# The output phase of a hybrid trunk: norms as 2 KB pieces, and the input added through PSUM by ScalarE

## The chip, the cores and the metric

One core of a Trainium2 chip runs the whole program. The time is that of the device, in microseconds (us), the median of several runs: lower is better. The engines are PE (TensorE: matmuls; PEld its weight loads), DVE (VectorE), ACT (ScalarE), POOL (GpSimd) and SP (SyncE, which here issues nearly all DMAs, in order). Each engine works through its own queue in order, and waits at an instruction whose inputs or buffers aren't ready; what stands behind it waits as well.

## What is computed

One layer over 2048 positions of width 1024, all in float32:

```
h    = rmsnorm(x);  proj = h @ w_in                 # split into u_b u_c u_h z xbc dt
y_a  = u_b * conv3(u_c * u_h)                       # short convolution mixer, 1024 wide
y    = ssd_scan(conv4(xbc), dt) + d_skip * xs       # chunked state-space scan, 16 heads
y_b  = rmsnorm over each of 2 groups of 512 (y * silu(z))
x    = x + concat(y_a, y_b) @ w_out                 # the output phase
x    = x + square(relu(rmsnorm(x) @ w_up)) @ w_down
out  = rmsnorm(x)
```

The change is in the line of the output phase, and in how the norms of y_b come to it.

## The kernel before

Everything lies transposed: 128 channels on the partitions, positions along the free axis. The 2048 positions are 4 blocks b of 512, the 1024 output channels 8 tiles d of 128. Matmuls work on float32r operands split into a high and a low part, so each product of a weight block and an activation block is three matmuls of 512 columns (L118 to L120 in `mm3`, L315 to L317 in `chain`).

**Pairs.** The half of the output projection that takes y_a comes first. `Output.pair(p)` for p = 0 to 7 computes two output tiles for two position blocks at once, c11, c12, c21 and c22, by the seven products of a Strassen-Winograd scheme instead of eight. Each product (b11, t1, t2, b21, t3, b22, t4, in this order) is 4 blocks of 3 matmuls. They accumulate in three PSUM banks: b11 goes to bank x and is copied by ACT into bank w (the copy `pw<-px`, L322), t1 goes to bank y, t2 adds to x, b21 adds to w, t3 adds to x, b22 adds to y, t4 adds to x. So t3 may not start until x has been read after t2, t4 not until it has been read after t3, and the next pair's t1 takes the bank that t4 filled. Banks x and y come in turn from the three banks k0, k1 and k2, bank w is k3.

After a product, `evict` (in `pair`) reads the bank. Before the pair, `begin` has loaded four tiles of the input x (`xt<-x`, `facc<-x`, L1602; 256 KB each); the six evictions add the bank to these tiles on DVE (L1627), the sums go out to x1_d in DRAM (`x_d<-xt`, `x_d<-facc`, L1630). The tiles of pair 0 come from a pool of the phase before (`begin(0, ...)` in `second_half`). The buffers are three of tag xt and two of tag facc.

**Units.** The half that takes y_b follows: `Output.unit(n)` for n = 32 to 63, one output tile d of one block b each, 8 k-blocks of 3 matmuls into one bank `pm` (in turn k0, k1, k2). The unit before has loaded x1_d for it (`residual`, `xt<-x_d`, L1658); DVE adds (L1679) and the result goes back to x1_d (L1680). For blocks 0 and 1 ACT squares the result (L1692) for the next norm.

**The scan beside it.** During the pairs and the first 16 units the state-space scan of blocks 2 and 3 is still running, a generator whose steps the function `hook` takes after every product and twice per unit: loads (`xd`, `bc`, `dec`, `eb`, `y`), transposes on PE (`ptx`, `ptb`), the copy `xtok<-ptx` (L1418) and the cast `xtok<-stmp` (L1434) on ACT, eight decays per chunk on ACT (`dec`, L1433), and so on. So the scan's instructions stand in the same queues as the pairs' and units'. `dec` is a broadcast of 512 KB from rd_d, `eb` two broadcasts of 128 KB each. The order on each engine is the program's, rearranged in places by the framework's scheduler before the kernel is built.

**The norms.** When a block and group of the scan is done, four small matmuls (`pn`, L1488) sum the squares over 512 channels; each of the block's four chunks of 128 positions gets its own 32 partitions, all with the same sums. ACT and DVE make the reciprocal root r of 128 x 128, and the whole tile is stored to rn_d (`rn_d<-ssq`, L1494; 64 KB). `norm` reads it back (`rn<-rn_d`, L1511): from rows 0, 32, 64 and 96 of rn_d, 512 bytes each, broadcast to 128 partitions (256 KB). `scale` multiplies y_b by it (L1571), `fill` splits it (ACT L1580, DVE L1581), each at a place of `hook` that `schedule` fixes by hand: for the four blocks the loads are at places 46, 54, 70 and 93 (7 places per pair, then 2 per unit with unit n at 2n).

Of the kernel before, what the change touches and what calls it, by code (L numbers as in the profile page):

```python
# [11 lines left out]
F32 = mybir.dt.float32  # L12
# [28 lines left out]
def trunk(ctx: ExitStack, tc: tile.TileContext, x, w_in, w_dt, w_out, w_up, w_down, cvec, hrow, out):  # L41
# [19 lines left out]
    ym_d = seven("ym")  # L61
    wide = lambda n, k: [dram.tile([P, k, TH], F32, name=f"{n}_d{h}") for h in range(2)]
    xs_d, sz_d, yn_d = wide("xs", 12), wide("sz", 8), wide("yn", 8)
    rn_d = [[dram.tile([P, L], F32, name=f"rn_d{b}_{g}") for g in range(G)] for b in range(NB)]
    dt_d = [dram.tile([P, 4, NC * 16], F32, name=f"dt_d{b}") for b in range(NB)]
    rd_d = [dram.tile([2, NC * 16, P], F32, name=f"rd_d{b}") for b in range(NB)]
    pd_d = dram.tile([P, TB], F32, name="pd_d")
# [406 lines left out]
    class Proj(Seven):  # L474
# [429 lines left out]
        def second_half(self, ws, side, stack):  # L904

            self.dt_open()
            dts = itertools.chain(*(self.dt_part(NBB + bb) for bb in range(NBB)))
            count = itertools.count()
            for m, what in enumerate(self.LATER):
                last = m + 1 == len(self.LATER)  # L910
                if m + 2 == len(self.LATER):
                    for _ in side:
                        pass
                    stack.close()
                    rb = stack.enter_context(tc.tile_pool(name="rb", bufs=1, reuse_waits="tile"))
                    self.fresh = lambda n: rb.tile([P, 2, TB], F32, tag="rb", name=n, bufs=4)
                    self.stored = ym_d
                    self.new = [{} for _ in range(4)]
                if last:
                    sums_d["o0"] = "none"  # L920
                    ahead = self.pairs(w_out[0], (0, 1), "o0", True)
                else:
                    ahead = self.weights(1, self.LATER[m + 1])

                def after(name):
                    if m or name == "t4":
                        next(dts, None)
                    for _ in range(1 + (next(count) % 3 == 2)):
                        next(side, None)
                    if m + 2 == len(self.LATER) and name == "t3":  # L930
                        self.got = self.fetch(0, 0)
                    if last:
                        if name == "t1":
                            next(ahead)
                        if name != "b11":
                            self.refresh(name, 0)
                        if name == "b22":
                            proj_out.begin(0, lambda tag: rb.tile([P, TB], F32, tag="xt", name="xt", bufs=4))

                ws = self.pair(1, what, ws, ahead, after)  # L940
            self.places = self.new
            return ws
# [396 lines left out]
    class Scan:  # L1339
# [104 lines left out]
        def back(self, n):  # L1444

            b, g, c, h, ts, r0 = self.place(n)
            t = self.got.pop(n)
            cT = t["bc"][:, 1]
            byhead = lambda a: a.rearrange("p (h d) -> p h d", h=HG)
            state = self.state[g]  # L1450
            st = psum("tp", "st", 2)
            mm3(st, *t["btok"], *t["parts"], 0, 1)
            yo = psum("k4", "yo")
            for j in range(4):
                nc.tensor.matmul(yo[:, j * L : (j + 1) * L], state[:, j * P : (j + 1) * P], cT, start=True, stop=True)
            yd = t["yd"]
            for i in range(HG):
                nc.tensor.matmul(
                    yd[(i % 2) * 64 : (i % 2) * 64 + 64, (i // 2) * L : (i // 2 + 1) * L],
                    byhead(t["xdt"])[:, i, :],  # L1460
                    t["dec"][:, i % 2 * 4 + i // 2, :],
                    start=False,
                    stop=True,
                    skip_group_check=True,
                )
            y = t["y"]
            t1 = self.tmp()
            nc.vector.tensor_tensor(out=byhead(state), in0=byhead(state), in1=t["cdec"], op=ALU.mult)
            nc.vector.tensor_tensor(out=state, in0=state, in1=st, op=ALU.add)
            nc.vector.tensor_tensor(out=t1, in0=yo, in1=t["eb"].rearrange("p j l -> p (j l)"), op=ALU.mult)  # L1470
            nc.vector.tensor_tensor(out=t1, in0=t1, in1=yd, op=ALU.add)
            yield
            t3 = t1.rearrange("p (j l) -> p j l", j=4)
            nc.vector.tensor_tensor(out=y, in0=t3, in1=y, op=ALU.mult)
            yield
            nc.sync.dma_start(yn_d[h][:, 4 * g : 4 * g + 4, ts], y)
            q4 = self.tmp().rearrange("p (j l) -> p j l", j=4)
            self.act = nc.scalar.activation(q4, y, AF.Square)
            nc.vector.tensor_tensor(out=q4[:, 0:2], in0=q4[:, 0:2], in1=q4[:, 2:4], op=ALU.add)
            if c == 0:  # L1480
                self.ssq = self.tile([TB], "ssq", 1)
            ssq = self.ssq
            nc.vector.tensor_tensor(out=ssq[:, c * L : (c + 1) * L], in0=q4[:, 0], in1=q4[:, 1], op=ALU.add)
            yield
            if c == NC - 1:
                pn = psum("tp", "pn", 2)
                for i in range(NC):
                    nc.tensor.matmul(  # L1488
                        pn[i * 32 : i * 32 + 32, 0:L], ones[:, 0:32], ssq[:, i * L : (i + 1) * L], start=True, stop=True
                    )  # L1490
                r = ssq[:, 0:L]
                nc.scalar.activation(r, pn[:, 0:L], AF.Sqrt, bias=eps, scale=1.0 / 512)
                nc.vector.reciprocal(out=r, in_=r)
                nc.sync.dma_start(rn_d[b][g], r)  # L1494
            yield
            yield

# [2 lines left out]
        def norm(self, b, g):  # L1500

            if (b, g) not in self.rn:
# [4 lines left out]
                else:  # L1507
                    t = uh.tile([P, TB], F32, tag="uh3", name="rn", bufs=4)
                self.rn[b, g] = t
                row = rn_d[b][g].rearrange("(q p) l -> p q l", p=32)[0]  # L1510
                nc.sync.dma_start(t.rearrange("p (q l) -> p q l", q=NC), row.partition_broadcast(P))  # L1511
            return self.rn[b, g]

        def run(self, begin, end):
# [34 lines left out]
    class Output:  # L1549
# [34 lines left out]

        def open(self, stack, ws):
            self.xp = stack.enter_context(tc.tile_pool(name="xp", bufs=1, reuse_waits="tile"))
            self.xt = {}
            self.start_ws = ws
            proj.fresh = self.raw

# [1 line left out]
            return self.xp.tile([P, 2, TB], F32, tag="ry", name=name, bufs=4)  # L1592

        def small(self, tag):
            return self.xp.tile([P, TB], F32, tag=tag, name=tag, bufs={"xt": 3, "facc": 2}[tag])

        def begin(self, p, tile=None):

            t = self.begun = {}
            for name, (b, i, tag) in self.TILES.items():  # L1600
                t[name] = (tile or self.small)(tag)
                nc.sync.dma_start(t[name], x[p // 4 * 2 + b, :, p % 4 * 2 + i])  # L1602

        def pair(self, p, hook):

            tiles = self.begun
            last = p == 7
            if p == 3:
                proj.new = [{} for _ in range(4)]
# [5 lines left out]
                ahead = proj.pairs(w_out[0], (d, d + 1), f"o{p + 1}", True)  # L1615

            def evict(name, gi, pm):
                for c, acc, end in {
                    "t1": (("c22", "y", 0),),
                    "t2": (("c12", "x", 0),),  # L1620
                    "b21": (("c11", "w", 1),),
                    "t3": (("c22", "x", 1),),
                    "b22": (("c12", "y", 1),),
                    "t4": (("c21", "x", 1),),
                }.get(name, ()):
                    t = tiles[c]
                    nc.vector.tensor_tensor(out=t, in0=pm[acc], in1=t, op=ALU.add)  # L1627
                    if end:
                        b, i, _ = self.TILES[c]
                        nc.sync.dma_start(x1_d[p // 4 * 2 + b][:, p % 4 * 2 + i], t)  # L1630

            def after(name):
                n = ("b11", "t1", "t2", "b21", "t3", "b22", "t4").index(name)
                if name == "b22":
                    if last:
                        self.residual(32)
                    else:
                        self.begin(p + 1)
                if p == 2 and name == "t4":
                    proj.got = proj.fetch(0)  # L1640
                if p == 3:
# [12 lines left out]
        def residual(self, n):  # L1654
            if n < len(self.UNITS):
                i, b, d = self.UNITS[n]
                t = self.xt[n] = self.small("xt")
                nc.sync.dma_start(t, x1_d[b][:, d])  # L1658

        def weights(self, m):  # L1660
            if m < 2 * KD and m not in self.ws:
                self.ws[m] = split_src(w_out[1, m % KD])

        def unit(self, n, hook):
# [3 lines left out]
            m = b // 2 * KD + d  # L1668
            if b % 2 == 0:
                self.weights(m + 2)  # L1670
            pm = psum("mm", "pm")
            whi, wlo = self.ws[m]
            for j in range(KD):
                if j == KD // 2:
                    hook(2 * n)
                k = j // 2 + j % 2 * 4
                mm3(pm, whi[:, k, :], wlo[:, k, :], *self.y[i, b][k], j, KD)
            t = self.xt.pop(n)
            nc.vector.tensor_tensor(out=t, in0=pm, in1=t, op=ALU.add)  # L1679
            nc.sync.dma_start(x1_d[b][:, d], t)  # L1680
# [38 lines left out]
    with ExitStack() as c1:  # L1719
# [17 lines left out]
        with ExitStack() as c2:  # L1737
# [13 lines left out]

            for p in range(8):
                proj_out.pair(p, hook)
            for n in range(32, 48):
                proj_out.unit(n, hook)
            for _ in side:
# [95 lines left out]
```

## Time and profile before

| | |
|---|---|
| median of 3 runs | 2622.15 us (2621.07 to 2628.47) |
| the profiled execution | 2623.34 us, of it the span 2621.6 us |
| mean granted PE clock | 0.993 |
| PE busy over the span | 2577.2 us (98%) |
| DVE, ACT busy over the span | 1946.4 us (74%), 1408.8 us (54%) |
| output phase, pairs (first to last eviction) | 970.9 to 1164.1 us |
| output phase, units (first to last addition) | 1181.2 to 1376.5 us |

Busy time is the time in which an engine executes; a wait shows as idle time, and the view names what ended it. PE's clock is granted by the chip, 1.00 being full speed.

### The profile page before, as it was taken

To read this page: it belongs to the slowest core of one execution; us is meant where nothing else is said; L and a number is where in the kernel's file an instruction comes from. 1 tells how busy PE (TensorE), PEld (TensorE's weight loads), DVE (VectorE), ACT (ScalarE), POOL (GpSimd) and SP (SyncE) were. 2 spreads that over 40 slices of the span, in tenths; PEclk is the share of its full clock that TensorE was granted. 3 is DMA by queue.
4 is the path that set the end of the run, shared out by engine and by line. 5 is a ranking of instruction groups with operands and counts; after the bars stand their busy time and mean duration, and the time that the engine had idled before them with its cause. 6 is when DMAs were issued, how large, how long until landed. Compare 5 with 4: busy or idle time off the path is not lost.

```text
span 2621.6 us, 33756 instructions
## 1 busy us (share of the span) xinstructions
PE 2577.2 (98%) x12027; PEld 2115.4 (81%) x12027; DVE 1946.4 (74%) x2651; ACT 1408.8 (54%) x2135; POOL 77.1 (3%) x99
## 2 busy tenths in 40 slices
PE   9999999999999999979999999999999999999998
PEld 7888878788888777767788888888888888888787
DVE  7877877878786778977777775744448887888885
ACT  6554345876676656554335555755556444444443
POOL 2110010000000000000000000000000000000001
PEclk9999999999999999989999999999999999999999
DMA  4555665756656478887666786765557554665762
GB/s 171 176 189 189 218 231 196 230 188 202 191 180 197 152 276 264 285 232 233 206 209 240 258 317 245 261 229 181 212 186 258 183 182 154 213 208 180 236 209 77
DMA packets 263016, 553.35 MB, mean 211 GB/s; under 512 B 27072, under 2 KB 99520, under 8 KB 262848
## 3 DMA queue, kind: packets, MB, share of 16 engines
q1 hardware_dynamic: 262272, 550.29, 62.4%
q8 instruction: 94, 1.54, 0.2%
q10 hardware_dynamic: 576, 0.92, 0.1%
q14 instruction: 74, 0.61, 0.1%
HBM read 364.20 MB, written 186.91 MB: 210 GB/s over the span
## 4 chain that ended last, share of the span: by engine, by line
PE 77%; DMA 7%; DVE 7%; ACT 5%; issue 3%; SPq 0%; POOL 0%; POOLq 0%; DVEq 0%; ACTq 0%
PE px L315 13%; PE px L317 13%; PE px L316 13%; PE py L315 6%; PE py L316 6%; PE py L317 6%; PE pw L315 3%; PE pw L317 3%; PE pw L316 3%; DMA dec<-rd_d 3%; PE pm L118 2%; PE pm L120 2%; PE pm L119 2%; ACT dec L1433 1%; DVE wlo L104 1%
## 5 line engine op out<-in xcount | busy, mean ns | idle before, releaser
L315 PE MATMUL px<-uh,whi 128*128 128x512 f32 x1800 | 705.8, 392 | 7.9 <-DVE xt L1627 2.4
L317 PE MATMUL px<-uh,wlo 128*128 128x512 f32 x1800 | 701.3, 390 | 0.0
L316 PE MATMUL px<-ul,whi 128*128 128x512 f32 x1800 | 701.0, 389 | 0.0
L315 PEld LDWEIGHTS px<-uh,whi 128*128 128x128 f32 x1800 | 337.9, 188 | 86.8 <-issue 4.1
L317 PEld LDWEIGHTS px<-uh,wlo 128*128 128x128 f32 x1800 | 337.9, 188 | 72.5 <-issue 2.2
L316 PEld LDWEIGHTS px<-ul,whi 128*128 128x128 f32 x1800 | 338.1, 188 | 68.9 <-issue 0.2
L104 DVE TENSOR_TENSOR wlo<-wraw,whi 128x512 fp32r<-128x512 f32 (+1 forms) x213 | 217.0, 1019 | 206.5 <-ACT whi L103 205.5
L315 PE MATMUL py<-uh,whi 128*128 128x512 f32 x900 | 353.0, 392 | 3.1 <-DVE facc L1627 2.6
L317 PE MATMUL py<-uh,wlo 128*128 128x512 f32 x900 | 351.4, 390 | 0.0
L316 PE MATMUL py<-ul,whi 128*128 128x512 f32 x900 | 351.3, 390 | 0.0
L103 ACT CAST whi<-s 128x1024 fp32r<-128x1024 f32 x226 | 236.5, 1047 | 204.8 <-PE py L316 86.8
L103 ACT CAST whi<-wraw 128x1024 fp32r<-128x1024 f32 (+1 forms) x214 | 190.5, 890 | 278.0 <-PE px L316 224.1
L104 DVE TENSOR_TENSOR wlo<-s,whi 128x1024 fp32r<-128x1024 f32 x226 | 275.1, 1217 | 80.3 <-ACT whi L103 79.7
L315 PEld LDWEIGHTS py<-uh,whi 128*128 128x128 f32 x900 | 169.4, 188 | 42.2 <-issue 5.7
L317 PEld LDWEIGHTS py<-uh,wlo 128*128 128x128 f32 x900 | 169.4, 188 | 35.4 <-issue 0.2
L316 PEld LDWEIGHTS py<-ul,whi 128*128 128x128 f32 x900 | 169.3, 188 | 35.4 <-issue 0.8
L315 PE MATMUL pw<-uh,whi 128*128 128x512 f32 x450 | 176.3, 392 | 0.0
L317 PE MATMUL pw<-uh,wlo 128*128 128x512 f32 x450 | 175.3, 390 | 0.0
L316 PE MATMUL pw<-ul,whi 128*128 128x512 f32 x450 | 175.1, 389 | 0.0
L391 DVE TENSOR_TENSOR ul<-rh,uh 128x1024 fp32r<-128x1024 f32 (+1 forms) x128 | 138.7, 1087 | 33.1 <-ACT uh L390 32.9
L390 ACT CAST uh<-rh 128x1024 fp32r<-128x1024 f32 (+1 forms) x128 | 120.3, 943 | 74.6 <-PE py L317 60.5
L118 PE MATMUL pm<-uh,whi 128*128 128x512 f32 (+1 forms) x392 | 150.2, 384 | 0.7 <-ACT z L601 0.7
(264 smaller groups left out, 3599.1 us busy)
## 6 DMA issues: line engine op xcount, KB each, us to landing
hid_d<-e SPq DMA_DIRECT2D x96, 512.0 KB, 3.5
rh<-hid_d SPq DMA_DIRECT2D x96, 512.0 KB, 4.3
wraw<-w_in SPq DMA_DIRECT2D x68, 512.0 KB, 4.2
wraw<-w_down SPq DMA_DIRECT2D x104, 256.0 KB, 3.5
wraw<-w_up SPq DMA_DIRECT2D x48, 512.0 KB, 4.8
dec<-rd_d SPq DMA_DIRECT2D x32, 512.0 KB, 5.2
wraw<-w_out SPq DMA_DIRECT2D x32, 512.0 KB, 5.4
sums_d<-s SPq DMA_DIRECT2D x32, 512.0 KB, 4.6
```

The costliest lines, as they stand in the source:

```text
L103: nc.scalar.copy(hi, raw)
L104: split["last"] = eng.tensor_tensor(out=lo, in0=raw, in1=hi.bitcast(F32), op=ALU.subtract)
L118: nc.tensor.matmul(out, whi, hi, start=(k == 0), stop=False)
L119: nc.tensor.matmul(out, whi, lo, start=False, stop=False)
L120: nc.tensor.matmul(out, wlo, hi, start=False, stop=(k == nk - 1))
L315: nc.tensor.matmul(p, hi, h[0], start=not seeded and k == 0, stop=False, **kw)
L316: nc.tensor.matmul(p, hi, h[1], start=False, stop=False, **kw)
L317: nc.tensor.matmul(p, lo, h[0], start=False, stop=(k == len(g) - 1), **kw)
L390: nc.scalar.copy(p[i][0], t)
L391: nc.vector.tensor_tensor(out=p[i][1], in0=t, in1=p[i][0].bitcast(F32), op=ALU.subtract)
L1433: nc.scalar.activation(dec[:, i], dec[:, i], AF.Relu, bias=t["a"][:, i : i + 1], scale=-1.0)
```

## The change

Two things are changed, and a third follows from them.

1. rn_d is a tile of 4 x 128 instead of 128 x 128. The store takes only partitions 0, 32, 64 and 96 of r; the load reads the 512 numbers as one piece of 2 KB, broadcast to 128 partitions.
2. The pairs no longer load or add x. The first bank of each output tile is copied by ACT (c22 after t1, c12 after t2, c11 after b21, c21 after t4), the second addition of c22 and c12 stays on DVE (after t3 and b22); what is stored to x1_d is the product alone. `begin` and its 32 loads are gone; the four buffers of pair 0 are now those of the other pairs.
3. x enters in the units: `origin` loads the tile of x into the one buffer `xr`, `seed` copies it on ACT into the next unit's bank, in the middle of the unit before, and asks for the load after that. The unit's 24 matmuls then all add to the bank. `seed(32)` stands between the last pair and the first unit, its load at b22 of the last pair.

```diff
-    rn_d = [[dram.tile([P, L], F32, name=f"rn_d{b}_{g}") for g in range(G)] for b in range(NB)]
+    rn_d = [[dram.tile([NC, L], F32, name=f"rn_d{b}_{g}") for g in range(G)] for b in range(NB)]
...
-                            proj_out.begin(0, lambda tag: rb.tile([P, TB], F32, tag="xt", name="xt", bufs=4))
...
-                nc.sync.dma_start(rn_d[b][g], r)
+                nc.sync.dma_start(rn_d[b][g], r.rearrange("(q p) l -> p q l", p=32)[0])
...
-                row = rn_d[b][g].rearrange("(q p) l -> p q l", p=32)[0]
-                nc.sync.dma_start(t.rearrange("p (q l) -> p q l", q=NC), row.partition_broadcast(P))
+                nc.sync.dma_start(t, rn_d[b][g].rearrange("q l -> (q l)").partition_broadcast(P))
...
-        def begin(self, p, tile=None):
-
-            t = self.begun = {}
-            for name, (b, i, tag) in self.TILES.items():
-                t[name] = (tile or self.small)(tag)
-                nc.sync.dma_start(t[name], x[p // 4 * 2 + b, :, p % 4 * 2 + i])
...
             def evict(name, gi, pm):
...
+                b, i, tag = self.TILES[c]
+                if add:
                     t = tiles[c]
                     nc.vector.tensor_tensor(out=t, in0=pm[acc], in1=t, op=ALU.add)
-                    if end:
-                        b, i, _ = self.TILES[c]
-                        nc.sync.dma_start(x1_d[p // 4 * 2 + b][:, p % 4 * 2 + i], t)
+                else:
+                    t = tiles[c] = self.small(tag)
+                    nc.scalar.copy(t, pm[acc])
+                if add or i == 0 and b == 0 or c == "c21":
+                    nc.sync.dma_start(x1_d[p // 4 * 2 + b][:, p % 4 * 2 + i], t)
...
-                if name == "b22":
-                    if last:
-                        self.residual(32)
-                    else:
-                        self.begin(p + 1)
+                if name == "b22" and last:
+                    self.residual(32)
+                    self.origin(32)
...
+        def seed(self, n):
+            if n < len(self.UNITS):
+                pm = self.pm[n] = psum("mm", "pm")
+                nc.scalar.copy(pm, self.res.pop(n))
+                self.origin(n + 1)
+
+        def origin(self, n):
+            if n < len(self.UNITS):
+                _, b, d = self.UNITS[n]
+                t = self.res[n] = self.small("xr")
+                nc.sync.dma_start(t, x[b, :, d])
...
-            pm = psum("mm", "pm")
+            pm = self.pm.pop(n)
             whi, wlo = self.ws[m]
             for j in range(KD):
                 if j == KD // 2:
+                    self.seed(n + 1)
                     hook(2 * n)
                 k = j // 2 + j % 2 * 4
-                mm3(pm, whi[:, k, :], wlo[:, k, :], *self.y[i, b][k], j, KD)
+                hi, lo = self.y[i, b][k]
+                w, v = whi[:, k, :], wlo[:, k, :]
+                nc.tensor.matmul(pm, w, hi, start=False, stop=False, skip_group_check=True)
+                nc.tensor.matmul(pm, w, lo, start=False, stop=False, skip_group_check=True)
+                nc.tensor.matmul(pm, v, hi, start=False, stop=(j == KD - 1), skip_group_check=True)
...
+            proj_out.seed(32)
             for n in range(32, 48):
                 proj_out.unit(n, hook)
```

More of the change, by code (lines that the diff above doesn't have):

```diff
@@ L1586, in open @@
             self.xp = stack.enter_context(tc.tile_pool(name="xp", bufs=1, reuse_waits="tile"))
-            self.xt = {}
+            self.xt, self.res, self.pm = {}, {}, {}
             self.start_ws = ws
@@ L1594, in small @@
         def small(self, tag):
-            return self.xp.tile([P, TB], F32, tag=tag, name=tag, bufs={"xt": 3, "facc": 2}[tag])
-        def begin(self, p, tile=None):
-            t = self.begun = {}
-            for name, (b, i, tag) in self.TILES.items():
-                t[name] = (tile or self.small)(tag)
-                nc.sync.dma_start(t[name], x[p // 4 * 2 + b, :, p % 4 * 2 + i])
+            return self.xp.tile([P, TB], F32, tag=tag, name=tag, bufs={"xt": 3, "facc": 2, "xr": 1}[tag])
         def pair(self, p, hook):
-            tiles = self.begun
+            tiles = {}
             last = p == 7
@@ L1617, in evict @@
             def evict(name, gi, pm):
[L1618 to L1625, printed above, removed]
+                c, acc, add = {
+                    "t1": ("c22", "y", 0),
+                    "t2": ("c12", "x", 0),
+                    "b21": ("c11", "w", 0),
+                    "t3": ("c22", "x", 1),
+                    "b22": ("c12", "y", 1),
+                    "t4": ("c21", "x", 0),
+                }.get(name, ("", "x", 0))
+                if not c:
+                    return
+                b, i, tag = self.TILES[c]
+                if add:
                     t = tiles[c]
                     nc.vector.tensor_tensor(out=t, in0=pm[acc], in1=t, op=ALU.add)
-                    if end:
-                        b, i, _ = self.TILES[c]
-                        nc.sync.dma_start(x1_d[p // 4 * 2 + b][:, p % 4 * 2 + i], t)
+                else:
[3 more added lines that the diff above has]
+                    nc.sync.dma_start(x1_d[p // 4 * 2 + b][:, p % 4 * 2 + i], t)
             def after(name):
                 n = ("b11", "t1", "t2", "b21", "t3", "b22", "t4").index(name)
-                if name == "b22":
-                    if last:
-                        self.residual(32)
-                    else:
-                        self.begin(p + 1)
+                if name == "b22" and last:
+                    self.residual(32)
+                    self.origin(32)
                 if p == 2 and name == "t4":
```

## The prediction

> **What bounds the kernel now.** I read the page first, then the busy times in stretches of 20 us over the output phase, the chain of waits of each engine there, the queue of SP, and the DMA view.
>
> ```profile
> span 2621.6 us, 33756 instructions
> PE 2577.2 (98%) x12027; PEld 2115.4 (81%) x12027; DVE 1946.4 (74%) x2651; ACT 1408.8 (54%) x2135; POOL 77.1 (3%) x99
> ```
>
> The profiled execution took 2623.34 us, so 1.7 us lie around its span; it is 1.2 us above the median of 2622.15 us. TensorE (PE) is busy for 98%, so only 44 us of the span are idle PE, and an edit that adds or removes no matmul can only gain that, plus clock that was not granted. The change touches the output phase. Its pairs run from the first eviction at 970.9 us to the last at 1164.1 us (first and last start below, between the columns of durations in ns and of forms); its 32 plain units follow.
>
> ```profile
> L1627 DVE TENSOR_TENSOR xt<-px,xt x17: 675/685/694, 970.9 to 1158.4; 128x512 f32<-128x512 f32 x17
> L1627 DVE TENSOR_TENSOR facc<-px,facc x7: 683/685/692, 1013.4 to 1164.1; 128x512 f32<-128x512 f32 x7
> ```
>
> In the stretches (us, then busy PE, PEld, DVE, ACT, POOL with instruction counts, granted clock, DMA share, GB/s) the loss is concentrated:
>
> ```profile
> 1120.00:1140.00 20.00, 16.90 (x92) 13.57 (x90) 14.98 (x25) 4.19 (x8) 0.00 (x0) 1.00 0.76 203
> 1140.00:1160.00 20.00, 19.29 (x91) 15.40 (x92) 18.13 (x27) 13.97 (x25) 0.00 (x0) 0.91 0.77 203
> 1160.00:1180.00 20.00, 9.80 (x45) 7.39 (x44) 10.52 (x16) 9.47 (x19) 0.00 (x0) 0.74 0.84 273
> ...
> 1220.00:1240.00 20.00, 17.50 (x78) 13.86 (x77) 18.02 (x27) 11.00 (x24) 0.00 (x0) 0.83 0.77 238
> 1240.00:1260.00 20.00, 18.09 (x90) 14.51 (x89) 12.62 (x20) 9.42 (x19) 0.00 (x0) 0.91 0.48 163
> ...
> 1320.00:1340.00 20.00, 20.00 (x90) 16.57 (x89) 17.87 (x27) 5.94 (x7) 0.00 (x0) 1.00 0.78 249
> ...
> sum 500.00, PE 474.48 PEld 384.90 DVE 395.18 ACT 253.28 POOL 2.13; mean PE 18.98 PEld 15.40 DVE 15.81 ACT 10.13 POOL 0.09
> ```
>
> From 900 to 1400 us PE is idle for 500 - 474.48 = 25.5 us. The clock not granted is 20 x (0.09 + 0.26 + 0.17 + 0.09) = 12.2 us in the four stretches below 1.00, and about 3 of that fall into idle time (by the step below). So about 25.5 + 9 = 34.5 us, 1.3% of the time, is all that can be won here. An undisturbed stretch runs 90 matmuls in 20 us, 0.222 us each: a product of a pair (12 matmuls) is 2.7 us, a plain unit (24) 5.3 us.
>
> Who PE waits for between 920 and 1390 us (total, times, longest):
>
> ```profile
> PE pn L1488 <- ACT xtok L1418: 10.2, 1, 10.2
> PE st L118 <- ACT xtok L1434: 6.2, 5, 2.3
> PE py L315 <- DVE facc L1627: 2.6, 1, 2.6
> PE px L315 <- DVE xt L1627: 2.4, 2, 1.2
> ...
> PE px L315 <- ACT pw L322: 1.0, 1, 1.0
> ```
>
> One wait of 10.2 us makes 40% of the idle time. Its cause is found by going backwards in the orders of ACT and SP:
>
> ```profile
> 1174.27 0.65 PE L1488 MATMUL pn<-ssq,ones_r 128*32 128x128 f32 x8 [10.20 <-ACT xtok L1418]
> ```
>
> ```profile
> 1169.41 0.40 ACT L1433 ACTIVATE dec<-dec,dd 128x128 f32<-128x128 f32 x1 [8.79 <-DMA dec<-rd_d]
> ```
>
> ```profile
> 1119.89 1.14 SPq L1511 DMA_DIRECT2D rn<-rn_d  x2
> ...
> 1121.62 6.03 SPq L1378 DMA_DIRECT2D bc<-xs_d  x2
> ...
> 1136.74 0.33 SPq L1602 DMA_DIRECT2D facc<-x  x1
> ...
> 1146.88 1.21 SPq L1511 DMA_DIRECT2D rn<-rn_d  x2
> 1149.14 4.41 SPq L98 DMA_DIRECT2D wraw<-w_out  x2
> 1153.82 5.07 SPq L1630 DMA_DIRECT2D x_d<-facc  x1
> ...
> 1159.63 0.82 SPq L1382 DMA_DIRECT2D dec<-rd_d  x1
> ```
>
> ACT stood 8.79 us for the decay rows; the copy xtok that PE needed is behind them. Their load was issued at 1159.63 us, because SP needed 4.41 and 5.07 us for issues that elsewhere take 0.3 to 0.6. Both follow directly on two norm loads, and at 1119.89 us the same pair of loads is followed by an issue of 6.03 us. In the DMA view of the pairs (960 to 1180 us: count, KB each, us to landing) the norm loads stand out; and of the two totals the first is that stretch, the second the 9 us from 1152 to 1161:
>
> ```profile
> DMA packets 39355, 58.63 MB, mean 266 GB/s; under 512 B 3108, under 2 KB 21284, under 8 KB 39339
> ...
> facc<-x SPq DMA_DIRECT2D x14, 256.0 KB, 4.3
> ...
> y<-sz_d SPq DMA_DIRECT2D x9, 256.0 KB, 4.2
> eb<-rd_d SPq DMA_DIRECT2D x18, 128.0 KB, 4.9
> ...
> rn<-rn_d SPq DMA_DIRECT2D x4, 256.0 KB, 10.9
> ```
>
> ```profile
> DMA packets 1029, 1.08 MB, mean 120 GB/s; under 512 B 52, under 2 KB 843, under 8 KB 1026
> ```
>
> Behind the norm loads the engines move 120 GB/s where the phase has 266, with 843 of 1029 packets under 2 KB. Small pieces alone don't do it (y also moves 512 B pieces, in 4.2 us), nor does broadcasting alone (eb broadcasts contiguous 2 KB rows, in 4.9 us). The norm load does both at once, with its four pieces 16 KB apart in DRAM.
>
> **The change, part by part.**
>
> *Norms.* The store shrinks from 128 pieces to 4, the load from 512 packets to 128, of the form that eb has. I take eb's 4.9 us as the landing instead of 10.9. What that is worth on PE: the slow issues after 1146.88 us disappear, so the decay load goes out some 6 to 9 us earlier and lands before 1174.27 - 10.20 = 1164.07 us, when PE began to wait. Gain 10.2 us, plus the clock: 0.74 over 20 us is 10.4 us at half speed; the last of these, an estimate of 4 us after PE had resumed, cost 2. What is late next is ACT's own work in front of xtok (eight decays and casts, some microseconds that the trace shows behind the landing); I take 1.0 back. Bounds: nothing, if the landing stays late, to 15.4 us (10.2 and the whole 5.2 of clock). Term: -11.2 us.
>
> *Pairs.* 32 loads of the input disappear here (256 KB each), and of 48 additions on DVE 32 become copies on ACT: 32 x 0.685 = 21.9 us of DVE work leaves, 8 pairs lose 2.7 us each. ACT gains 32 copies from PSUM; the nearest row is the copy pw, also PSUM and of the same size:
>
> ```profile
> 1144.40 0.58 ACT L322 COPY pw<-px 128x512 f32<-128x512 f32 x1
> ```
>
> That is 18.6 us in some 200, on an engine that is busy for 4 to 14 of 20 us in the stretches above: hidden, as work. The waits of PE for L1627 go, 2.6 + 2.4 = 5.0 us; the 2.6 came from c21's input, loaded only at 1136.74 us, and was followed by a clock of 0.91, 1.8 us. Term: -6.8. In their place PE now waits for ACT's copies: after t2 it has 2.7 us (b21) until t3 adds to the same bank, after t4 2.7 us (the next b11). Behind a decay row that is late, ACT misses that. The one such copy that exists, pw, has 2.7 us too and cost 1.0 us in 8 pairs; two new ones per pair at its price give +2.0. Bounds: 0 (DVE's lighter queue serves the scan sooner) to 5.0 (as many waits as DVE had) and, if a gap throttles, 1.8 more.
>
> *Units.* Each gains a copy from SBUF into PSUM on ACT and a load of 256 KB; the additions stay. The copy's nearest row is the square that ACT writes into PSUM:
>
> ```profile
> L1692 ACT ACTIVATE sq<-xt x14: 582/602/603, 1195.2 to 1294.3; 128x512 f32<-128x512 f32 x14
> ```
>
> 32 x 0.60 = 19 us hide under an ACT that is half idle. New is a wait: the first matmul of a unit needs its seed, and the seed is in ACT's queue behind the scan's work, and its one input buffer (xr) makes SP hold the next load until ACT has read the last; stores, scan loads and weights are queued behind that on SP. Two waits measure the exposure, ACT's for the scan's xd and SP's at the residual load:
>
> ```profile
> ACT yd L1440 <- DMA xd<-xs_d: 13.8, 3, 9.4
> ```
>
> ```profile
> SPq L1658 <- DMA x_d<-xt: 74.7, 26, 7.4
> xt<-x_d SPq DMA_DIRECT2D x32, 256.0 KB, 3.3
> ```
>
> A seed is asked for in the middle of the unit before, and its bank is free a unit earlier, so an ACT that is stuck for up to about 5.3 us costs nothing; the 9.4 us one would cost about 4. I take +3.0 over the units; bounds 0 and the case below. The remaining idle time of the units (2.5 and 1.9 us by the stretches, and their clock) I leave as it is; it may as well vanish or double.
>
> The sum: -11.2 - 6.8 + 2.0 + 3.0 = -13.0 us. From 2623.3 that gives 2610.3 for the profiled execution, and 1.2 less, 2609 us, for the median.
>
> **Rivals.** *The pieces were not the cause.* The landing of 10.9 us could be a queue that is full of bytes: a share of 0.76 to 0.84 speaks for it, 120 GB/s speaks against. Then the 10.2 us stall stays, evictions and seeds give -6.8 + 2.0 + 3.0 = -1.8, and the time is 2620. The Trainium skill, DMA: Bandwidth & Descriptors, Specifications, says that transfers of at least 512 B already run at line rate. By that rule norms of 512 B lose nothing to size and this rival is what would come; the trace has 512 B packets that are fast (y) and slow (rn), so it does not support the rule for this broadcast. A variant with the same outcome: the stall is cured, but ACT's copies at t2 and t4 stall PE by about as much.
>
> *The seeds become a loop.* Seed, next load's issue, landing, next seed: 0.60 + 2.9 (74.7 / 26, SP at the residual load just ahead of it) + 3.3 = 6.8 us. Units with scan work last longer than that on average; the 16 after the scan last 5.3. If nothing of it overlaps, these lose 16 x 1.5 = 24 us, and -16.0 + 24 = +8: 2630. It decides when seeds are late by over 16 us in all, 0.5 us a unit; slower needs 24. Against it: SP's wait for the last store runs while PE is in the unit, the seed has up to two units of lead, and the DMA share of the quoted stretch after the scan is 0.78, with a median landing of 3.3 us.
>
> *All goes.* With fewer stalls the rest of the phase unclogs, too: the xtok waits (6.2) and the units' clock (5.2). -18 - 11.4 from the median gives 2593.
>
> **How the numbers follow.** The forecast, -8 to -18 us, has 0.50; pieces not the cause or a stall moved to ACT 0.22; the loop of seeds 0.14; all goes 0.14. 0.3%, 7.9 us, is about what a measurement tells from no change, so faster means below 2614.3: 0.63 (forecast and "all goes", less 0.01 for the forecast's edge); same 0.23; slower 0.14. The range reaches from 2597 (most of "all goes") to 2625 (the second case whole, the loop in part).
>
> **What would show it.** Right: norm loads landing near 5 us, no SP issue of over 4 us behind them, no wait of PE at pn, clock 1.00 from 1140 to 1180 us. PE waits for L1627 gone, waits for the new copies under 3 us. Seeds: PE at pm waiting for ACT under 5 us in all. Wrong: norm loads that still land late (first term), PE waiting at px or py for ACT by 5 us or more (second), or PE idle at the start of most units after the scan, with SP waiting for ACT at the new load (third).

## The result, and the profile after

The changed kernel took 2605.3 us (median of 4 runs, 2605.0 to 2608.5); beside it, the kernel before had a median of 2625.3 us over 4 runs. The ratio is 0.9927 with a 95% interval of 0.9907 to 0.9948: about 19 us faster, where 13 were forecast. The two profiled executions stand at 2623.34 and 2605.26 us. The runs below were made on three chips, each beside the kernel before, whose median there was 2625.8 to 2628.1 us; their ratios to it compare better than their medians do.

The page's first lines, after:

```profile
span 2603.5 us, 33796 instructions
PE 2570.4 (99%) x12027; PEld 2110.9 (81%) x12027; DVE 1928.4 (74%) x2619; ACT 1438.0 (55%) x2199; POOL 74.7 (3%) x99
```

Idle PE fell from 44 to 33 us; the remaining 7 us of the 18 are clock, which shows as shorter busy time with the same 12027 matmuls. The stretches of 20 us after (columns as in the prediction):

```profile
1120.00:1140.00 20.00, 20.00 (x106) 16.25 (x105) 14.31 (x22) 10.99 (x24) 0.00 (x0) 1.00 0.55 167
1140.00:1160.00 20.00, 17.48 (x102) 14.09 (x101) 16.86 (x25) 13.70 (x26) 0.00 (x0) 1.00 0.92 307
1160.00:1180.00 20.00, 20.00 (x106) 16.41 (x105) 19.06 (x26) 16.06 (x29) 0.00 (x0) 1.00 0.80 253
...
1220.00:1240.00 20.00, 20.00 (x108) 16.63 (x107) 15.27 (x24) 12.45 (x24) 0.00 (x0) 1.00 0.81 260
...
1340.00:1360.00 20.00, 15.57 (x67) 12.20 (x66) 14.42 (x15) 12.06 (x14) 0.00 (x0) 0.98 0.44 148
```

The stalls and the low clock around 1130, 1165 and 1230 us are gone. What is left at 1140 us is the wait at pn below. The stretch at 1340 us, where the units end, has a new hole. The waits of PE between 920 and 1390 us (total, times, longest):

```profile
PE px L315 <- DVE xt L1691: 4.1, 1, 4.1
PE pn L1486 <- ACT xtok L1416: 2.5, 1, 2.5
PE pm L1687 <- ACT pm L1658: 2.5, 4, 1.3
PE st L118 <- ACT xtok L1432: 2.4, 2, 1.5
PE py L315 <- ACT facc L1625: 1.1, 1, 1.1
```

The wait of 10.2 us at pn is down to 2.5. The seeds (`pm`, L1658) cost 2.5 directly and ACT's eviction copies (L1625) 1.1, both near what I had expected. The 4.1 us at the top are a wait that I hadn't thought of. In the DMA view of 960 to 1180 us the norm load lands like its neighbour eb:

```profile
eb<-rd_d SPq DMA_DIRECT2D x20, 128.0 KB, 5.0
...
rn<-rn_d SPq DMA_DIRECT2D x4, 256.0 KB, 5.2
```

All traces have 12027 matmuls, so the start of the n-th one marks the same place in the work, and the time between two such places compares kernels stage by stage even where the absolute times have shifted. (Among the pairs, the order differs a little between kernels; at the bounds chosen here the same matmuls have been done, but for six at the end of the pairs in the table's last row.) I use four stages: the pairs (matmul 4650 to 5550), the end of the pairs with the units that run beside the scan (to 6000), the units behind the scan (to 6450), and the end of the units with the first products of the next phase (to 6600). In us, one profiled execution each:

| kernel | pairs | with scan | behind it | end |
|---|---|---|---|---|
| before | 186.0 | 107.3 | 100.8 | 34.3 |
| changed | 179.0 | 89.2 | 102.2 | 40.7 |
| changed, second execution | 180.1 | 93.2 | 100.8 | 39.5 |
| norms only | 185.9 | 88.0 | 100.8 | 34.3 |
| products only | 185.9 | 103.1 | 109.6 | 41.0 |
| norms, 512 B, 1 KB apart | 184.7 | 90.7 | 100.8 | 34.3 |
| norms, 512 B, 16 KB apart, 4 rows stored | 187.4 | 109.5 | 100.8 | 34.3 |
| norms, 512 B, 4 KB apart | 187.5 | 95.5 | 100.8 | 34.3 |
| no seeds | 176.5 | 88.5 | 100.8 | 34.3 |
| seeds from one tile | 177.4 | 87.2 | 100.8 | 34.3 |
| last four units unseeded | 178.5 | 91.6 | 101.5 | 34.6 |
| input loads on ACT's queue | 178.8 | 97.6 | 100.8 | 40.3 |
| evictions copied by DVE | 180.3 | 94.8 | 100.8 | 41.3 |
| last pair keeps the input | 181.9 | 85.5 | 100.8 | 34.7 |

The two executions of the changed kernel differ by 4 us in the second stage, so differences of that size there mean little. The values 100.8 and 34.3 recur because PE waits for nothing there.

### The profile page after: what moved, and what is told of

Its sections match the earlier page's. It is cut to its first block, busy times and chain, and to the rows that moved or that the text cites. A ratio compares the mean times of both kernels' runs of the same rounds, so it can differ in the third digit from the quotient of the medians.

```text
span 2603.5 us, 33796 instructions
## 1 busy us (share of the span) xinstructions
PE 2570.4 (99%) x12027; PEld 2110.9 (81%) x12027; DVE 1928.4 (74%) x2619; ACT 1438.0 (55%) x2199; POOL 74.7 (3%) x99
## 4 chain that ended last, share of the span: by engine, by line
PE 78%; DVE 7%; DMA 7%; ACT 4%; issue 3%; SPq 0%; POOL 0%; POOLq 0%; DVEq 0%; ACTq 0%
PE px L315 14%; PE px L316 14%; PE px L317 14%; PE py L315 7%; PE py L316 7%; PE py L317 7%; PE pw L315 3%; PE pw L317 3%; PE pw L316 3%; DMA dec<-rd_d 1%; DMA xr<-x 1%; DVE ul L391 1%; PE yd L1456 1%; ACT dec L1431 1%; DVE wlo L104 1%
## 5 line engine op out<-in xcount | busy, mean ns | idle before, releaser
L322 ACT COPY pw<-px 128x512 f32<-128x512 f32 x115 | 65.8, 573 | 125.9 <-PE px L317 125.5
```

The costliest lines, as they stand in the source:

```text
L322: nc.scalar.copy(pm[gi]["w"], pm[gi]["x"])
```

## The experiments

**The norms alone.** To the kernel before, the three norm edits of the change's diff, nothing else.

> The kernel before with the norm part alone (2 KB pieces); the pairs still load and add the input on VectorE. Theory A, the pieces: the norm loads land in about 5 us instead of 10.9, no issue of SP behind them takes over 4 us, the 10.2 us wait before pn is gone, and most of the gain is here: 11 to 15 us, a ratio of 0.9943 to 0.9958. Theory B, the traffic: what unclogged the pairs is that the 32 input loads left them, so the norms alone give under 4 us, a ratio above 0.9985.

Measured: 2604.5 us, ratio 0.9914 (0.9896 to 0.9931). This is the whole gain of the change, and more than theory A gave to the norms. Theory B is out. PE's waits in this run:

```profile
PE px L315 <- ACT pw L322: 4.5, 2, 2.7
PE st L118 <- ACT xtok L1434: 3.1, 3, 1.8
PE pn L1488 <- ACT xtok L1418: 1.8, 1, 1.8
```

In SP's queue one of the two long rows that the prediction blamed on the norm loads is still there, and the other isn't:

```profile
1149.08 4.40 SPq L98 DMA_DIRECT2D wraw<-w_out  x2
1153.74 0.33 SPq L1629 DMA_DIRECT2D x_d<-facc  x1
1154.88 0.56 SPq L1564 DMA_DIRECT2D ry<-yn_d  x1
1155.53 0.55 SPq L1382 DMA_DIRECT2D dec<-rd_d  x1
```

The 4.40 us of the two weight loads are no effect of slow norms, and no long issue either. The row joins two issues of 0.33 us, and between them SP waits for DVE to free the buffer of the weights:

```profile
SPq L98 <- DVE wlo L104: 5.2, 2, 3.6
```

The kernel before has the same wait of 3.6 us there. The 5.07 us of the store behind them, a single issue, did come from the norms: it takes 0.33 now, so the decay load goes out 4 us earlier than before, and it lands faster, too. ACT begins the decays at 1161.81 us instead of 1169.41, and PE waits 1.81 us:

```profile
1161.81 0.40 ACT L1433 ACTIVATE dec<-dec,dd 128x128 f32<-128x128 f32 x1 [1.25 <-DMA dec<-rd_d]
```

```profile
1166.68 0.43 PE L1488 MATMUL pn<-ssq,ones_r 128*32 128x128 f32 x8 [1.81 <-ACT xtok L1418]
```

**The products alone.** The changed kernel with the three norm edits undone.

> The changed kernel with the norms as before (four 512-byte rows out of 128). Theory A: norm loads land near 11 us again, a wait of PE for the scan of several us is back, and the gain is 2 to 6 us, a ratio of 0.9977 to 0.9992. Theory B: the gain is nearly whole, over 14 us, a ratio below 0.9947.

Measured: 2635.7 us, ratio 1.0032 (1.0020 to 1.0045). The products alone make the kernel slower, which neither theory expected. PE's first waits:

```profile
PE pm L1688 <- ACT pm L1659: 8.7, 3, 6.4
PE pn L1486 <- ACT xtok L1416: 8.0, 1, 8.0
PE ptx L1411 <- DMA xd<-xs_d: 5.9, 2, 4.5
```

With slow norm loads PE waits 8.7 us for seeds, 6.4 of it at once, at 1299.5 us. There the seed's own tile isn't late. DVE waits for the last norm load, ACT's cast waits for DVE, and the seed stands behind this cast:

```profile
1292.18 1.41 DVE L1569 SCALAR_TENSOR_TENSOR ry<-ry,cv,rn 128x512 f32<-128x512 f32 x2 [6.42 <-DMA rn<-rn_d]
```

```profile
1293.02 1.04 ACT L1578 CAST uh<-ry 128x1024 fp32r<-128x1024 f32 x1 [6.11 <-DVE ry L1569]
...
1298.90 0.57 ACT L1659 COPY pm<-xr 128x512 f32<-128x512 f32 x1
```

This is the coupling of PE to ACT's other waits that the prediction feared. With quick norms PE's wait for seeds shrinks to 2.5.

**Which property of the pieces is slow?** Three variants of the kernel before that change only how the norms lie. First, 512-byte pieces 1 KB apart:

```diff
-    rn_d = [[dram.tile([P, L], ...
+    rn_d = [[dram.tile([NC, 2 * L], ...
-                nc.sync.dma_start(rn_d[b][g], r)
+                nc.sync.dma_start(rn_d[b][g][:, 0:L], r.rearrange("(q p) l -> p q l", p=32)[0])
-                row = rn_d[b][g].rearrange("(q p) l -> p q l", p=32)[0]
+                row = rn_d[b][g][:, 0:L]
```

> The kernel before with norms of 512-byte pieces still, but the four pieces 1 KB apart instead of 16 KB, and only four rows stored. If the number of packets (512 instead of 128) is what makes the norm load slow: landing stays near 11 us and the ratio above 0.998. If it is the 16 KB between the pieces: landing near 5 us as with 2 KB pieces and a ratio as in the run with the norms alone (0.994 to 0.996 by theory A).

Measured: 2606.5 us, 0.9918 (0.9896 to 0.9940). Then the load as before, but only the four rows stored:

```diff
-                nc.sync.dma_start(rn_d[b][g], r)
+                nc.sync.dma_start(rn_d[b][g].rearrange("(q p) l -> p q l", p=32)[0],
+                                  r.rearrange("(q p) l -> p q l", p=32)[0])
```

> The kernel before, its norms still loaded as four 512-byte pieces 16 KB apart, but only these four rows stored. If the distance of the pieces in the load is the cause: landing still near 10 us and the time as before within 3 us. If the store of 64 KB was the burden: landing near 5 us and 2604 to 2608.

Measured: 2627.4 us, 1.0003 (0.9989 to 1.0016). And the first variant with `8 * L`, pieces 4 KB apart:

> The kernel before with norms of 512-byte pieces 4 KB apart. At 1 KB they landed in 4.7 us, at 16 KB in 10.9. If any distance beyond the contiguous is fine up to some larger power of two: 5 us and 2604 to 2608; if the landing grows with the distance: 6 to 9 us and between.

Measured: 2613.2 us, 0.9946 (0.9927 to 0.9965). The norm loads in the DMA view of 1105 to 1290 us, at 1, 16 and 4 KB:

```profile
rn<-rn_d SPq DMA_DIRECT2D x8, 256.0 KB, 4.7
```

```profile
rn<-rn_d SPq DMA_DIRECT2D x8, 256.0 KB, 8.5
```

```profile
rn<-rn_d SPq DMA_DIRECT2D x8, 256.0 KB, 6.3
```

The x8 counts the issues; the trace of each variant tells the landing of only one of the eight, the same load in all three (the kernel before tells all eight, 7.7 to 14.9 us, and 8.2 for this one). So the landings are one sample each, and other figures have to bear them out. The last norm load stands alone in its stretch: there 512 packets of 512 bytes move in each variant, and in the packet records one takes 28, 39 and 149 ns on average. Two more come from SP's queue and from PE's waits:

| distance | SP's issue of the store behind the norm loads | PE's wait at pn | ratio |
|---|---|---|---|
| 1 KB | 0.33 us | 3.7 us | 0.9918 |
| 4 KB | 2.35 us | 6.4 us | 0.9946 |
| 16 KB, 4 rows stored | 4.97 us | 10.5 us | 1.0003 |
| 16 KB, kernel before | 5.07 us | 10.2 us | 1 |

All follow the distance, and so does the time. The size of the pieces isn't the cause, nor is the store. Joining them to 2 KB helps because joined pieces are near each other. All three distances are powers of two, and no run has one that isn't; so it isn't shown whether the distance counts as such or only such distances do.

**What the seeds cost.** First without them: no load of the input behind the pairs, and each unit's first matmul starts its bank (`start=(j == 0)`), so the input is missing from the result.

> The changed kernel without the input in the output phase: no load of it and no seed copy, the units' first matmul starts the bank (the residual addition of the input is left out). What the seeds cost in all. My term was 3.0 us, so the theory that seeds cost little gives 2 to 4 us below the changed kernel, 2601 to 2603. If the seeds' waits are also what delays ScalarE's casts at the end of the units and with them the first product behind, the 6 us that the changed kernel gives back there are won too: 2596 to 2599.

Measured: 2596.6 us, 0.9883 (0.9864 to 0.9902). By the medians the seeds cost 8.7 us against the changed kernel's 2605.3, by the ratios 11 to 12, and by the four stages 11.0. Of the last, the end of the units makes 6.4, the pairs 2.5. Then the copies without the loads, every seed from the tile of unit 32:

```diff
-                nc.scalar.copy(pm, self.res.pop(n))
-                self.origin(n + 1)
+                nc.scalar.copy(pm, self.res[32])
```

> The changed kernel with all 32 seed copies, but all from the one tile that unit 32 loads: no other load of the input (the wrong input tile is added to 31 output tiles). It keeps the copies and PE's wait for them and takes away the wait for the loads. If the loads' landing is what makes the seeds cost 8.7 us: 2596 to 2599, as without seeds. If ScalarE's copies themselves and their place in its queue cost it: 2603 to 2606.

Measured: 2599.5 us, 0.9896 (0.9878 to 0.9914), a profiled execution of 2593.4. Its stages are those without seeds, within a microsecond or so: 32 copies on ACT and PE's wait for them are free. What costs comes with the loads. This run takes away both their traffic and ACT's wait for them; the traces point to the wait, for ACT stands at a seed until its tile has landed. In the changed kernel, this is ACT's longest wait between 920 and 1390 us, 54.6 us in 19 times:

```profile
ACT pm L1658 <- DMA xr<-x: 54.6, 19, 8.6
```

How this reaches PE at the end of the units is seen in the timeline of the changed kernel, first ACT, then DVE, then PE:

```profile
1345.20 0.59 ACT L1658 COPY pm<-xr 128x512 f32<-128x512 f32 x1 [2.53 <-DMA xr<-x]
1345.72 3.89 ACT L390 CAST uh<-first 128x1024 fp32r<-128x1024 f32 x4
```

```profile
1358.29 0.69 DVE L1691 TENSOR_TENSOR xt<-pm,xt 128x512 f32<-128x512 f32 x1
```

```profile
1359.03 0.69 PE L315 MATMUL px<-uh,whi 128*128 128x512 f32 x1 [4.06 <-DVE xt L1691]
```

The four casts for the next phase run back to back as soon as the last seed is copied; none waits for anything of its own, so they had been ready before. With the norms alone, each of these casts is released by PE, as here the first:

```profile
1342.15 1.05 ACT L390 CAST uh<-first 128x1024 fp32r<-128x1024 f32 x1 [0.53 <-PE pm L120]
```

DVE's subtractions follow the casts, its last addition stands behind them, and the next phase's product into `px` needs the bank which that addition frees. If so, it is the last seeds that matter. Units 60 to 63 were left without load and seed (their four tiles lack the input):

```diff
+BARE = 60
...
-                nc.scalar.copy(pm, self.res.pop(n))
+                if n < BARE:
+                    nc.scalar.copy(pm, self.res.pop(n))
...
         def origin(self, n):
-            if n < len(self.UNITS):
+            if n < BARE:
...
-                nc.tensor.matmul(pm, w, hi, start=False, stop=False, skip_group_check=True)
+                nc.tensor.matmul(pm, w, hi, start=(n >= BARE and j == 0), stop=False, skip_group_check=True)
```

> The changed kernel without load and seed for units 60 to 63 alone (the input is left out of these four output tiles). Theory E, the last seeds hold up ScalarE's casts for the next phase, and these VectorE's last addition, for which the first product behind the units waits: that wait of 4.1 us goes and with its clock loss 5 to 7 us are won of the 8.7 that all seeds cost, 2598 to 2600. Rival, each of the 32 seeds costs its share: 4/32 of 8.7, 1 us, 2604.

Measured: 2602.2 us, 0.9904 (0.9889 to 0.9919). In the trace PE's wait is gone, and the end of the units takes 34.6 us instead of 40.7:

```profile
PE px L316 <- DVE xt L1693: 0.2, 1, 0.2
```

The total lies between the two forecasts: 3 us below the changed kernel by the medians, 6 by the ratios, whose intervals overlap. The stage and the wait carry the verdict.

Two more figures of the traces bear it out. ACT still waits 44.8 us for the tiles of the other units in this run, and PE only 1.1 us for their seeds, so neither a wait of ACT nor a load costs much by itself. And measured from the 6450th matmul, the first of the four casts starts 2.3 us before it with the norms alone, 1.3 us after it here, and 6.1 us after it in the changed kernel; PE's wait at px is 0, 0.2 and 4.1 us. The last seeds aren't all of this delay: with units 60 to 63 bare, ACT still stands 9.7 us at the next phase's load `lx<-x_d` just before the casts, and that uses up the slack. The two seeds that stand between this load and the casts in the changed kernel make the wait.

**SP's order or one buffer?** The changed kernel with the input's loads on ACT's queue:

```diff
                 t = self.res[n] = self.small("xr")
-                nc.sync.dma_start(t, x[b, :, d])
+                nc.scalar.dma_start(t, x[b, :, d])
```

> The changed kernel with the loads of the input tile xr issued from ScalarE's DMA queue, straight behind the seed that frees the buffer, instead of from SyncE's. Theory S, SyncE's order is what makes the seeds late (its issue of xr waits for ScalarE's seed, and stands behind stores and residual loads that wait): the wait of ScalarE for xr falls from 54.6 us to under 30, and 4 to 8 us are won, 2597 to 2601. Rival, one buffer is the limit (seed, load, landing, seed) whatever queue it is on: no change beyond 2 us.

Measured: 2612.8 us, 0.9943 (0.9927 to 0.9958): not faster, perhaps slower. ACT's wait for the tile fell less than theory S needed, and the end of the units kept its 40.3 us:

```profile
ACT pm L1658 <- DMA xr<-x: 41.9, 15, 6.0
```

SP's order isn't the main limit. That leaves the rival, one buffer in a circle of copy, issue and landing; no run has a second buffer, so this is not shown.

**ACT or DVE for the evictions?** The changed kernel with the four plain copies of a pair on DVE:

```diff
-                    nc.scalar.copy(t, pm[acc])
+                    nc.vector.tensor_copy(t, pm[acc])
```

> The changed kernel with the four plain evictions of a pair copied by VectorE instead of ScalarE; the input's loads stay out of the pairs. If moving the evictions to ScalarE is what won 6 to 8 us in the pairs (as against the norms alone), these are lost: 2611 to 2613. If the absent loads of the input won them, nothing changes beyond 2 us.

Measured: 2611.5 us, 0.9941 (0.9923 to 0.9959). The pairs take 180.3 us, as in the second execution of the changed kernel (180.1) and 5.6 less than with the norms alone. So what won 6 to 7 us in the pairs is that the input's loads left them, with the waits for them. ACT's wait for the decay loads fits: between 968 and 1150 us it is 11.9 us with the norms alone, 5.7 here and 5.6 in the changed kernel. The total is unclear: 2 to 6 us slower than the changed kernel by the medians, and what the stages show of it lies behind the pairs, where executions scatter.

**A version without the late seeds.** The four tiles whose units come last all belong to the last pair. If this pair alone loads and adds the input as the kernel before does, units 59, 61, 62 and 63 need no seed, and nothing is left out:

```diff
+        BARE = (59, 61, 62, 63)
...
-            tiles = {}
             last = p == 7
+            tiles = self.begun if last else {}
...
-                if add:
+                if add or last:
...
+                if name == "b22" and p == 6:
+                    self.begun = {}
+                    for c, (b, i, tag) in self.TILES.items():
+                        self.begun[c] = self.small(tag)
+                        nc.sync.dma_start(self.begun[c], x[2 + b, :, 6 + i])
...
-                nc.scalar.copy(pm, self.res.pop(n))
+                if n not in self.BARE:
+                    nc.scalar.copy(pm, self.res.pop(n))
```

(`origin` skips these units, and their first matmul starts the bank.) On the same chip the changed kernel ran again:

> The changed kernel itself, to be compared on the same chip with the next run: as before, a ratio of 0.992 to 0.994 to the kernel before.

> The changed kernel, whole in what it computes, but the last pair loads and adds the input on VectorE as the kernel before does, so that its four tiles' units (59, 61, 62, 63) need no load and no seed. Theory E: the wait of 4.1 us before the first product behind the units goes, 4 to 6 us against the changed kernel, 0.990 to 0.991 of the kernel before. Rival: the last pair's loads bring back in the pairs what they save at the end, no change beyond 2 us.

Measured: the changed kernel 2609.0 us, 0.9925 (0.9908 to 0.9942); this version 2601.9 us, 0.9904 (0.9886 to 0.9922), a profiled execution of 2597.98. The stretch around the end of the units, in the changed kernel's first profile and in this version's:

```profile
1335.00:1365.00 30.00, 25.57 (x105) 20.20 (x104) 19.98 (x24) 13.52 (x17) 0.00 (x0) 0.94 0.58 189
```

```profile
1335.00:1365.00 30.00, 29.68 (x131) 24.07 (x130) 23.29 (x28) 16.75 (x19) 0.00 (x0) 1.00 0.64 206
```

PE does 131 matmuls there instead of 105. The last pair's loads cost the pairs 2 to 3 us, by the table; the end gives 5 to 6 back. By its median this version is the fastest that computes everything, but its interval overlaps with those of the norms alone and of the change, so that it is faster in total is not shown.

## Why the prediction was right, and where not

The direction, the stage and the first stall were right, and the time lay in the range, 4 us below the forecast value; the gain of 19 us lay just beyond the 8 to 18 that the forecast gave. That the sum came out so near was luck in part: the norms gave about twice their term and the seeds cost about three times theirs, two errors of opposite sign. One reason was wrong as well.

*Norms, -11.2.* The place was right: the decay load, the wait at pn, the clock. The decay load went out 4 us earlier, though, not 6 to 9, and the wait shrank to 1.8 us. The term was too small. With the norms alone the stage beside the scan fell by 107.3 - 88.0 = 19.3 us, the kernel by about 22. I had priced one stall of 10.2 us and its clock and left the units' idle time and clock "as it is"; these were late effects of the same slow loads (two of the four pairs of norm loads fall into the units). The clock stretches of 0.83 and 0.91 there went to 1.00.

The reason that I gave was half wrong. "Small pieces alone don't do it, nor does broadcasting alone" was right, but then I took the number of packets for the cause, and named the 16 KB between the pieces in passing. The variants show the distance. The rule of the Trainium skill that I weighed was that transfers of 512 bytes already run at line rate (DMA: Bandwidth & Descriptors, Specifications). These runs agree in that size costs nothing here: 512-byte pieces 1 KB apart landed in 4.7 us, the joined ones with the norms alone in 5.7 (one landing each); what the line rate is, they don't show. The rival that I hung on it was wrong nevertheless, since the change removes the distance along with the size. I had also put two long issues of SP down to the norm loads. The row of 4.41 us is none: it joins two issues of 0.35 us with a wait of 3.6 us for DVE, and it stays when the norms are quick.

*Pairs, -6.8 + 2.0 = -4.8.* Measured against the norms alone: 185.9 to 179.0 us, 6.9 won (5.8 in the second execution). The direct wait for ACT's copies is 1.1 us where I took 2.0. But the move to ACT isn't what won it; with the copies on DVE the pairs take as long. The waits differ, too, from those that I had counted: with the norms alone PE waits only 1.1 us for DVE's evictions in the pairs and 4.5 us for ACT's copy pw, and it is this wait that is missing from the changed kernel's list.

*Seeds, +3.0.* This is the step that failed most: 9 to 12 us. PE's direct wait for a seed was as small as I had forecast (2.5 us), and I looked no further. On SP I had named what is queued behind the new wait; on ACT I had named only the scan's work in front of the seed, and so put what stands behind it at nothing. Behind the last seeds on ACT stand the casts for the next phase, and the bill is presented there, as a wait for DVE: 4.1 us, and behind it 3.4 us at a granted clock of 0.53. The loop of seeds that I had as a rival didn't come: the units behind the scan take 102.2 and 100.8 us in the two executions, 100.8 without seeds.

*The two parts together.* I gave the products -1.8. With the norms quick they are worth nothing that was measured (ratios of 0.9927 and 0.9914, with intervals that overlap); alone they cost 0.32%. The whole gain of the change is in the norms.

## What to carry to other kernels

Price a slow transfer by all that follows it in the queues, not by the one longest stall, and test a suspected property of it (size, number, distance) by changing that one alone. When a step is moved into an in-order queue, look for what stands behind it at the end of the phase too: there the first consumer of the next phase pays for a wait that the step's own row doesn't show. A change of two parts should be timed in its parts: here one carried everything and the other gave back in one stage what it won in another.

## What the hardware showed that I had not expected

A broadcast of four 512-byte rows to 128 partitions landed in 4.7, 6.3 and 8.5 us (one landing each) as the rows lay 1, 4 and 16 KB apart in DRAM, with packets of the same size and number. An issue of SP behind such loads took 0.33, 2.35 and 4.97 us. Why the distance matters no run shows, nor whether a distance that is no power of two would do the same. A load of 256 KB with that defect, eight times in the kernel, cost it about 20 us, since in-order queues stood behind it.
